# A longer stand-in between the second and third product for the state, in the first chunk of each head's scan

## The chip, the cores and the metric

The kernel runs on one core of a Trainium2 chip. The metric is the device time of one execution in microseconds (us), as a median of several runs. Engine names follow the profile: PE is the matrix engine, PEld its weight loads, DVE the vector engine, ACT the scalar engine, POOL the GpSimd engine, SP the engine that issues most DMAs.

## What is computed

A decoder trunk of two layers over 1024 tokens of width 1024. The first layer is a gated DeltaNet with 8 heads (key width 128, value width 256), the second a sliding-window attention that reads keys and values computed once. Only the first layer is touched here. Its core is a scan over chunks of the sequence that carries a state S:

```python
def step(S, inp):
    qk_i, qd_i, kd_i, u_i, w_i, gl_i = inp
    v_new = u_i - jnp.einsum("bhck,bhkv->bhcv", w_i, S)
    o = jnp.einsum("bhck,bhkv->bhcv", qd_i, S) + jnp.einsum("bhcs,bhsv->bhcv", qk_i, v_new)
    S = S * gl_i[..., None, None] + jnp.einsum("bhck,bhcv->bhkv", kd_i, v_new)
    return S, o
```

Everything around it in that layer is projection work: the layer's input, normalised, times the weights for queries, keys, values and a gate z, then a short convolution along the sequence, and at the end a product with the output weights.

## The kernel before

The sequence is cut into 8 chunks of 128 tokens. Factors of the scan and the projections are split into a high and a low part, and three products (high by high, low by high or high by low, and the other cross product) stand for one product in full precision.

The first layer goes head by head, heads 0 to 7. `head_delta` (L658) is the scan of one head. Its first half builds, for all 8 chunks at once, the inverse that the chunked form needs: products of keys with queries (L668), a mask, levels of small products (L700, L693), three corrections (L693), three merges (L762, L767, L772). Its second half is the loop over chunks n (L796 to L838): r from the state (L800, L802; not in the first chunk, which has no state yet), the new values from r (L809), their high part `vh` on ACT (L811) and their low part `vl` on DVE (L812, tile lh), three products for the new state (L820 and L821 with `vh`, L823 with `vl`), S itself on DVE (L829 in the first chunk, L826 later), its high and low parts (L831, L832). `inside` (L785; its products are L654 to L656, as are those of L815) computes the output of a chunk.

These steps form one long chain for a head, so the PE would stand idle between them. The kernel fills it: `head_delta` is a generator that yields, after each step, a number from the table `WAIT`, roughly the microseconds that its next step has to wait for the other engines. `interleave` (L86) then issues projection matmuls of the next head and of the gate (`gemm_ct`, lines L180, L182, L184, called fillers here) until their costs (0.215 to 0.22 each) add up to that number times `share`. `share` (L348) is the projection work of the head over `WAIT_SUM`, the sum of all that a head yields; so the number of fillers of a head is fixed, and the table only says how they are spread. Heads 5 and 6 leave their gate's projection to the end, and head 0 has half of its gate done earlier, so they have fewer fillers per step than heads 1 to 4 and 7.

The order on the PE is the order in which the program is written. On DVE, ACT, POOL and SP a scheduler sets the order from its own estimate of when each operation's inputs are there; each engine then runs its list strictly in order. On DVE the scan shares the list with the low parts of weights (L157), the three taps of a convolution (L494), the key norms (L589 to L591, L111 to L119), the sums for the queries (L546, L548), and the low parts of the decayed keys and of the decay (L648: tile lt and tile dml; the high parts are POOL's L647).

Of the kernel before, what the change touches and what calls it, by code (L numbers as in the profile page):

```python
# [24 lines left out]
NEG = -1.0e30  # L25
EPS = 1e-6

WAIT = {"kq": 0.7, "mask": 4.05, "level": 1.37, "fix": 2.05, "merge": 1.04, "row": 0.99, "new": 1.02, "state": 0.86, "low": 0.23}
WAIT_SUM = 4 * WAIT["kq"] + 1 * WAIT["mask"] + 10 * WAIT["level"] + 3 * WAIT["fix"] + 3 * WAIT["merge"] + 7 * WAIT["row"] + 8 * WAIT["new"] + 7 * WAIT["state"] + 7 * WAIT["low"]
LEVELS = (1, 2, 4, 8, 16, 32)  # L30

C_ID = 0
# [32 lines left out]
class Kernel:  # L65
# [190 lines left out]
    def layer_a(self):  # L256
        nc, tc, I = self.nc, self.tc, self.I
        with ExitStack() as ctx:
# [76 lines left out]
            for h in range(AH):  # L335
# [11 lines left out]
                spare = 0.99 if h in late else 6 if h + 1 == AH else 10  # L347
                share = (10.4 * blocks - spare) / WAIT_SUM  # L348
                self.interleave(self.head_delta(h, cur), self.chain(back), share)
# [308 lines left out]
    def head_delta(self, h, H):  # L658
        nc, dl, sm, dps = self.nc, self.dl, self.sm, self.dps
        kq, kt, vt, dm = H.kq, H.kt, H.vt, H.dm  # L660
# [3 lines left out]
        for n2 in range(NB // 2):  # L664
            ps = dps.tile([P, 2, 2, P], F32, name="kqp")
            for c in range(2):
                n = n2 * 2 + c
                nc.tensor.matmul(ps[:, c, :, :], kq[:, n, 0, :], kq[:, n, :, :], start=True, stop=True)  # L668
            for c in range(2):
                n = n2 * 2 + c  # L670
# [3 lines left out]
            nc.vector.tensor_tensor(out=dm[:, sl, :], in0=ps[:, :, 1, :], in1=dm[:, sl, :], op=ALU.mult)  # L674
            yield WAIT["kq"]

# [13 lines left out]
        def prod(lhs, rhs):  # L690
            ps = dps.tile(sh, F32, name="kqp")
            for n, r in blocks:
                nc.tensor.matmul(ps[r:r + 64, n, :], lhs(n, r), rhs(n, r), start=True, stop=True)  # L693
            return ps
# [8 lines left out]
        def part(t):  # L703
            return lambda n, r: t[r:r + 64, n, :]

        def const(j):
            return self.mskh[:, 64 * j:64 * j + 64].unsqueeze(1).broadcast_to(sh)

        def swap(name, t):
            o = sm.tile(sh, F16, name=name, bufs=1)  # L710
            nc.vector.transpose(out=o.rearrange("p n c -> p (n c)"), in_=t.rearrange("p n c -> p (n c)"))
            return o
# [7 lines left out]
        XT = swap("XT", X)  # L720
        yield WAIT["mask"]
        pair = [P, 2, NB, 64]
        w = sm.tile(pair, F32, name="w0", bufs=1)
        Xf, XTf = w[:, 0], w[:, 1]
        for lv, b in enumerate(LEVELS[1:], 2):
            y = whole(self.lh, X)
            Z = sm.tile(sh, F16, name="Z", bufs=1)
            nc.vector.tensor_tensor(out=Z, in0=y, in1=const(lv), op=ALU.mult)
            yield WAIT["level"]
            px = prod(part(XT), part(Z))  # L730
# [3 lines left out]
            else:  # L734
                pxt = prod(part(Z), part(XT))
                nc.vector.tensor_tensor(out=Xf, in0=px, in1=X, op=ALU.add)
                nc.vector.tensor_tensor(out=XTf, in0=pxt, in1=XT, op=ALU.add)
            yield WAIT["level"]

# [6 lines left out]
        for t in (Eh, Ef):  # L746
            nc.vector.tensor_tensor(out=t, in0=y, in1=Ef, op=ALU.add)
        yield WAIT["fix"]
        y = prod(part(Eh), part(XTh))
# [35 lines left out]
        def inside(n):  # L785

            self.three(po[n % 2][:, 1, :], dmh[:, n, :], dml[:, n, :], vh, vl)
            if n:
                nc.vector.tensor_tensor(out=o[:, n, :], in0=po[n % 2][:, 1, :], in1=o[:, n, :], op=ALU.add)
            else:  # L790
                nc.scalar.copy(out=o[:, n, :], in_=po[n % 2][:, 1, :])
            junk = sm.tile([P, 256], BF16, name="junk2", bufs=1)
            nc.scalar.activation(out=junk, in_=o[:, n, :], func=AF.Square, accum_out=sso[:, n:n + 1])

        S = None
        for n in range(NB):  # L796
            po[n % 2] = dps.tile([P, 2, 256], F32, name="kqp")
            if n:
                ps = dps.tile([P, 512], F32, name="sc")[:, 0:256]
                nc.tensor.matmul(ps, kq[:, n, 0, :], S, start=True, stop=True)  # L800
                r = sm.tile(wide, F32, name="r")
                nc.vector.scalar_tensor_tensor(out=r, in0=ps, scalar=self.neG[:, n, h:h + 1], in1=vt[:, n, :],  # L802
                                               op0=ALU.mult, op1=ALU.add)
                inside(n - 1)
                yield WAIT["row"]
            else:
                r = vt[:, n, :]
            ps = dps.tile([P, 512], F32, name="sc")[:, 0:256]
            nc.tensor.matmul(ps, xt[:, n, :], r, start=True, stop=True)  # L809
            beta = self.beta[:, n, h:h + 1]  # L810
            nc.scalar.activation(out=vh, in_=ps, func=AF.Copy, scale=beta)  # L811
            nc.vector.scalar_tensor_tensor(out=vl, in0=ps, scalar=beta, in1=self.f32(vh), op0=ALU.mult,  # L812
                                           op1=ALU.subtract)
            if n:
                self.three(po[n % 2][:, 0, :], qh[:, n, :], ql[:, n, :], Sh, Sl)  # L815
                nc.scalar.activation(out=o[:, n, :], in_=po[n % 2][:, 0, :], func=AF.Copy, scale=self.eG[:, n, h:h + 1])
            yield WAIT["new"]
            if n < NB - 1:
                ps = dps.tile([P, 512], F32, name="sc")[:, 0:256]
                nc.tensor.matmul(ps, kth[:, n, :], vh, start=True, stop=False)  # L820
                nc.tensor.matmul(ps, ktl[:, n, :], vh, start=False, stop=False)  # L821
                yield WAIT["low"]
                nc.tensor.matmul(ps, kth[:, n, :], vl, start=False, stop=True)  # L823
                S2 = sm.tile(wide, F32, name="S")
                if n:
                    nc.vector.scalar_tensor_tensor(out=S2, in0=S, scalar=self.egl[:, n, h:h + 1], in1=ps,  # L826
                                                   op0=ALU.mult, op1=ALU.add)
                else:
                    nc.vector.tensor_copy(S2, ps)  # L829
                S = S2  # L830
                nc.scalar.copy(out=Sh, in_=S)  # L831
                nc.vector.tensor_tensor(out=Sl, in0=S, in1=self.f32(Sh), op=ALU.subtract)  # L832

                if n < 4:
                    (part_d, part_k, part_d, part_d)[n](some[(0, 1, 1, 2)[n]])
                if n == 2:
                    part_k(some[2])
                yield WAIT["state"]  # L838
# [560 lines left out]
```

## Time and profile before

| | |
|---|---|
| median of 3 runs | 1867.74 us (1866.12 to 1868.64) |
| the profiled execution | 1867.72 us |
| its span, first to last instruction | 1866.0 us |
| scans of the 8 heads, in the span | about 99 us to 890 us |
| PE busy in the span | 97% |

The profile comes from one execution, of 1867.72 us; 1.7 us of it lie outside the span. In rows of the timeline the first two numbers are the start in us from the span's start and the length; a row with xN is N equal instructions in one piece, and [1.19 <-DVE lh L812] says that the engine stood idle for 1.19 us before it, until DVE's L812 released it. Idle time under about 0.2 us has no bracket.

### The profile page before, as it was taken

How to read it: one execution, taken by the hardware profiler on the slowest of the kernel's cores; microseconds unless marked ns; L12 is line 12 of the kernel's file. 1: busy time of each engine (PE TensorE's matmuls, PEld its weight loads, DVE VectorE, ACT ScalarE, POOL GpSimd, SP SyncE). 2: the span in 40 equal slices, each digit the busy share in tenths (PEclk: the TensorE clock that was granted, in tenths of full speed). 3: DMA queues.
4: the chain of work that ended last, by engine and by line, in shares of the span. 5: the costliest groups of instructions: out<-in, count | busy, mean ns of one | idle time of the engine just before them, and what ended most of it. 6: DMA issues, size and time to landing. Idle time of an engine off the chain costs nothing.

```text
span 1866.0 us, 31106 instructions
## 1 busy us (share of the span) xinstructions
PE 1809.7 (97%) x11778; PEld 1466.0 (79%) x11778; DVE 1231.2 (66%) x2895; ACT 730.7 (39%) x1813; POOL 514.0 (28%) x629
## 2 busy tenths in 40 slices
PE   6999999999999998999999999999999999999999
PEld 6667778787878776778788899887787787777887
DVE  6777776868586778765545365777776766763432
ACT  6446362634445364523112042444444444441100
POOL 1323232323222233221311231333333323221211
PEclk9999999999999999999999999999999999999999
DMA  4611111112011111122655331111111111225552
GB/s 151 134 49 35 57 46 46 47 35 69 23 58 35 58 34 47 45 91 92 236 170 171 122 92 46 30 46 46 63 41 52 57 34 59 68 69 201 182 169 102
DMA packets 134874, 149.55 MB, mean 80 GB/s; under 512 B 7242, under 2 KB 91716, under 8 KB 134724
## 3 DMA queue, kind: packets, MB, share of 16 engines
q1 hardware_dynamic: 124384, 130.40, 22.5%
q10 hardware_dynamic: 10340, 17.16, 2.9%
q8 instruction: 93, 1.52, 0.3%
q14 instruction: 57, 0.47, 0.1%
HBM read 116.05 MB, written 31.49 MB: 79 GB/s over the span
## 4 chain that ended last, share of the span: by engine, by line
PE 77%; DVE 10%; issue 3%; POOL 3%; ACT 1%; DMA 1%; POOLq 0%; DVEq 0%; ACTq 0%; SPq 0%
PE mm L180 9%; PE mm L182 9%; PE mm L184 9%; PE acc L933 6%; PE acc L932 6%; PE acc L931 6%; PE mm L983 4%; PE mm L984 4%; PE mm L985 4%; PE pv L1218 3%; PE lg L1174 3%; DVE acc L494 2%; PE tp L1197 1%; DVE wlo L157 1%; PE kqp L693 1%
## 5 line engine op out<-in xcount | busy, mean ns | idle before, releaser
L180 PE MATMUL mm<-hh,whi 128*128 128x512 f32 (+1 forms) x1040 | 428.0, 412 | 2.5 <-ACT hh L246 2.4
L182 PE MATMUL mm<-hl,whi 128*128 128x512 f32 (+1 forms) x1040 | 417.9, 402 | 1.5 <-DVE hl L247 1.5
L184 PE MATMUL mm<-hh,wlo 128*128 128x512 f32 (+1 forms) x1040 | 415.4, 399 | 0.0
L157 DVE TENSOR_TENSOR wlo<-wraw,whi 128x512 fp32r<-128x512 f32 x292 | 205.8, 728 | 225.0 <-POOL whi L150 192.4
L150 POOL TENSOR_SCALAR whi<-wraw 128x1024 fp32r<-128x1024 f32 x110 | 121.3, 1103 | 474.7 <-PE acc L933 240.7
L180 PEld LDWEIGHTS mm<-hh,whi 128*128 128x128 f32 x1040 | 197.0, 189 | 39.1 <-issue 4.6
L184 PEld LDWEIGHTS mm<-hh,wlo 128*128 128x128 f32 x1040 | 196.9, 189 | 37.3 <-issue 4.2
L182 PEld LDWEIGHTS mm<-hl,whi 128*128 128x128 f32 x1040 | 197.2, 190 | 35.6 <-issue 4.2
L983 PE MATMUL mm<-whi,hh 128*128 128x256 f32 x608 | 183.6, 302 | 0.0
L984 PE MATMUL mm<-wlo,hh 128*128 128x256 f32 x608 | 171.9, 283 | 0.0
L985 PE MATMUL mm<-whi,hl 128*128 128x256 f32 x608 | 171.8, 283 | 0.0
L494 DVE SCALAR_TENSOR_TENSOR acc<-u,cw,acc 128x512 f32<-128x512 f32 x192 | 152.9, 798 | 22.0 <-POOL acc L491 19.6
L1187 ACT ACTIVATE lsb<-lsb,m 128x129 f32<-128x129 f32 x256 | 100.4, 394 | 165.2 <-DVE m L1182 129.3
L983 PEld LDWEIGHTS mm<-whi,hh 128*128 128x128 f32 x608 | 115.8, 190 | 14.7 <-issue 10.0
L1191 POOL TENSOR_TENSOR lsb<-lsb,den 128x512 f32<-128x512 f32 x64 | 72.9, 1139 | 189.2 <-DVE den L1189 177.6
L153 POOL TENSOR_TENSOR wraw<-wraw,gcolb 128x512 f32<-128x512 f32 x72 | 79.0, 1117 | 140.4 <-DMA wraw<-in_b_w_in 96.7
L984 PEld LDWEIGHTS mm<-wlo,hh 128*128 128x128 f32 x608 | 116.1, 191 | 0.2
L985 PEld LDWEIGHTS mm<-whi,hl 128*128 128x128 f32 x608 | 115.8, 190 | 0.0
L491 POOL TENSOR_SCALAR acc<-u,cw 128x512 f32<-128x512 f32 x64 | 57.0, 891 | 183.4 <-ACT u L487 169.9
L931 PE MATMUL acc<-whi,hh 128*128 128x512 f32 x256 | 99.7, 389 | 0.0
L933 PE MATMUL acc<-whi,hl 128*128 128x512 f32 x256 | 99.6, 389 | 0.0
L932 PE MATMUL acc<-wlo,hh 128*128 128x512 f32 x256 | 99.6, 389 | 0.0
(352 smaller groups left out, 3722.0 us busy)
## 6 DMA issues: line engine op xcount, KB each, us to landing
wraw<-in_a_w_in SPq DMA_DIRECT2D x48, 512.0 KB, 4.0
wraw<-in_a_w_out SPq DMA_DIRECT2D x32, 512.0 KB, 3.6
wraw<-in_b_w_in SPq DMA_DIRECT2D x32, 512.0 KB, 4.0
wraw<-in_b_w_out SPq DMA_DIRECT2D x32, 512.0 KB, 3.9
og<-zs SPq DMA_DIRECT2D x32, 256.0 KB, 2.0
ogT<-zs SPq DMA_DIRECT2D x24, 256.0 KB, 2.1
btab<-lt SPq DMA_DIRECT2D x1, 4096.0 KB, 24.3
dm<-gd SPq DMA_DIRECT2D x8, 512.0 KB, 4.1
```

The lines of the kernel that those rows point to most:

```text
L150: nc.gpsimd.tensor_scalar(out=hi, in0=raw, scalar1=1.0, scalar2=1.0, op0=ALU.mult, op1=ALU.mult)
L157: nc.vector.tensor_tensor(out=lo[:, ks], in0=raw[:, ks], in1=self.f32(hi[:, ks]), op=ALU.subtract)
L180: nc.tensor.matmul(ps, hi[:, k, :], hh[:, k, :], start=(k == 0), stop=False)
L182: nc.tensor.matmul(ps, hi[:, k, :], hl[:, k, :], start=False, stop=False)
L184: nc.tensor.matmul(ps, lo[:, k, :], hh[:, k, :], start=False, stop=(k == KT - 1))
L494: nc.vector.scalar_tensor_tensor(out=acc, in0=u[:, t:t + 512], scalar=cw[:, t, blk:blk + 1], in1=acc, op0=ALU.mult, op1=ALU.add)
L931: nc.tensor.matmul(ps[c], oh[:, k, ts], hi[:, kk, :], start=(k4 + k == 0), stop=False)
L932: nc.tensor.matmul(ps[c], oh[:, k, ts], lo[:, kk, :], start=False, stop=False)
L933: nc.tensor.matmul(ps[c], ol[:, k, ts], hi[:, kk, :], start=False, stop=(k4 + k == 6))
L983: nc.tensor.matmul(ps, hh[:, k, ts], hi[:, k % 4, :], start=(k == 0), stop=False)
L984: nc.tensor.matmul(ps, hh[:, k, ts], lo[:, k % 4, :], start=False, stop=False)
L985: nc.tensor.matmul(ps, hl[:, k, ts], hi[:, k % 4, :], start=False, stop=(k == KT - 1))
```

## The change

`WAIT` gets a new entry, `low0` = 1.5. In the loop over chunks, between L821 and L823, the first chunk yields it instead of `low` = 0.23; the other six still yield `low`. `WAIT_SUM` counts 6 times `low` and once `low0`, so it goes from 52.54 to 53.81, and `share` falls by 2.4% in every head.

```diff
-WAIT = {..., "state": 0.86, "low": 0.23}
-WAIT_SUM = ... + 7 * WAIT["state"] + 7 * WAIT["low"]
+WAIT = {..., "state": 0.86, "low": 0.23, "low0": 1.5}
+WAIT_SUM = ... + 7 * WAIT["state"] + 6 * WAIT["low"] + WAIT["low0"]
...
                 nc.tensor.matmul(ps, kth[:, n, :], vh, start=True, stop=False)
                 nc.tensor.matmul(ps, ktl[:, n, :], vh, start=False, stop=False)
-                yield WAIT["low"]
+                yield WAIT["low" if n else "low0"]
                 nc.tensor.matmul(ps, kth[:, n, :], vl, start=False, stop=True)
```

Both programs hold the same instructions on every engine; they differ in order between head 0's scan and the end of head 7's, and nowhere else. Three places follow.

On the PE, head 5, first chunk, before: from the first product for the state to the first use of the state (L800). The operands are Z for `vh`, lh for `vl`, w_7089 and lt for the high and low part of the keys.

```order
L820 MATMUL sc<-Z,w_7089 128x256
L821 MATMUL sc<-Z,lt 128x256
L823 MATMUL sc<-lh,w_7089 128x256
L180 MATMUL mm<-hh_85,whi 128x512
L182 MATMUL mm<-hl_86,whi 128x512
L184 MATMUL mm<-hh_85,wlo 128x512
L800 MATMUL sc<-S,kq 128x256
```

The same place after:

```order
L820 MATMUL sc<-Z,w_7086 128x256
L821 MATMUL sc<-Z,lt 128x256
L180 MATMUL mm<-hh_85,whi 128x512
L182 MATMUL mm<-hl_86,whi 128x512
L184 MATMUL mm<-hh_85,wlo 128x512
L180 MATMUL mm<-hh_85,whi 128x512
L182 MATMUL mm<-hl_86,whi 128x512
L823 MATMUL sc<-lh,w_7086 128x256
L184 MATMUL mm<-hh_85,wlo 128x512
L180 MATMUL mm<-hh_85,whi 128x512
L182 MATMUL mm<-hl_86,whi 128x512
L800 MATMUL sc<-S,kq 128x256
```

Five fillers stand before L823 where there were none; three of them were taken from steps ahead of L820 (111 fillers of the head stood ahead of L820, now 108) and two from steps behind.

On DVE, head 5, the list up to the first state (L829), before:

```order
L157 TENSOR_TENSOR wlo<-wraw,whi 128x512
L591 TENSOR_TENSOR kt<-kt,rky 128x1024
L648 TENSOR_TENSOR lt<-kt,w_7089 128x256 x2
L648 TENSOR_TENSOR lt<-kt,w_7089 128x512
L648 TENSOR_TENSOR dml<-dm,w_7091 128x256 x2
L494 SCALAR_TENSOR_TENSOR acc<-u,cw,acc 128x512
L648 TENSOR_TENSOR dml<-dm,w_7091 128x512
L812 SCALAR_TENSOR_TENSOR lh<-sc,beta,Z 128x256
L494 SCALAR_TENSOR_TENSOR acc<-u,cw,acc 128x512
L829 COPY S<-sc 128x256
```

After:

```order
L591 TENSOR_TENSOR kt<-kt,rky 128x1024
L648 TENSOR_TENSOR lt<-kt,w_7086 128x256 x2
L648 TENSOR_TENSOR lt<-kt,w_7086 128x512
L648 TENSOR_TENSOR dml<-dm,w_7088 128x256 x2
L494 SCALAR_TENSOR_TENSOR acc<-u,cw,acc 128x512
L812 SCALAR_TENSOR_TENSOR lh<-sc,beta,Z 128x256
L494 SCALAR_TENSOR_TENSOR acc<-u,cw,acc 128x512
L648 TENSOR_TENSOR dml<-dm,w_7088 128x512
L829 COPY S<-sc 128x256
```

One L157 and the last L648 no longer stand ahead of L812; the L648 now stands between L812 and L829, the L157 behind L829.

On the PE, head 1 (heads 2 to 4 are the same), the merges, before; L596 turns the next head's keys:

```order
L762 MATMUL kqp<-cst,xt 64x64 x8
L180 MATMUL mm<-hh_87,whi 128x512
L182 MATMUL mm<-hl_88,whi 128x512
L184 MATMUL mm<-hh_87,wlo 128x512
L596 MATMUL tr<-cst,kt 128x128 x8
L180 MATMUL mm<-hh_87,whi 128x512
L182 MATMUL mm<-hl_88,whi 128x512
L767 MATMUL kqp<-w_2148,lt 64x64 x8
```

After:

```order
L762 MATMUL kqp<-cst,xt 64x64 x8
L182 MATMUL mm<-hl_88,whi 128x512
L184 MATMUL mm<-hh_87,wlo 128x512
L180 MATMUL mm<-hh_87,whi 128x512
L182 MATMUL mm<-hl_88,whi 128x512
L767 MATMUL kqp<-w_2147,lt 64x64 x8
L184 MATMUL mm<-hh_87,wlo 128x512
L596 MATMUL tr<-cst,kt 128x128 x8
```

L596 is behind L767 now, since it hangs on the number of fillers issued. On POOL, at the same place of head 1, before (L686 decays the next head's keys and waits for L596; L647 splits this head's keys and decay):

```order
L686 TENSOR_TENSOR kt<-kt,kdec 128x512 x2
L647 TENSOR_SCALAR w_2682<-kt 128x256 x2
L647 TENSOR_SCALAR w_2682<-kt 128x512
L647 TENSOR_SCALAR w_2684<-dm 128x256 x2
L647 TENSOR_SCALAR w_2684<-dm 128x512
```

After:

```order
L647 TENSOR_SCALAR w_2679<-kt 128x256 x2
L647 TENSOR_SCALAR w_2679<-kt 128x512
L686 TENSOR_TENSOR kt<-kt,kdec 128x512 x2
L647 TENSOR_SCALAR w_2681<-dm 128x256 x2
L647 TENSOR_SCALAR w_2681<-dm 128x512
```

L686 has moved from ahead of both splits to between them.

## Rows read from the trace of the kernel before

**Rows 1.** The page's head and first part: busy us, share of span, instructions

```profile
span 1866.0 us, 31106 instructions
PE 1809.7 (97%) x11778; PEld 1466.0 (79%) x11778; DVE 1231.2 (66%) x2895; ACT 730.7 (39%) x1813; POOL 514.0 (28%) x629
```

**Rows 2.** A stretch: length, busy us (PE, PEld, DVE, ACT, POOL), PEclk, DMA

```profile
750.00:755.00 5.00, 2.78 (x10) 2.27 (x10) 3.99 (x8) 2.21 (x3) 0.00 (x0) 0.76 0.61 206
```

**Rows 3.** The PE's waits over the span: us in total, times, longest us

```profile
PE sc L823 <- DVE lh L812: 10.8, 14, 2.2
```

**Rows 4.** Timeline of PE, first chunk: heads 0, 1, 5 (five rows), 6, 7

```profile
147.46 0.39 PE L823 MATMUL sc<-lh,w 128*128 128x256 f32 x1 [1.19 <-DVE lh L812]
...
251.40 0.37 PE L823 MATMUL sc<-lh,w 128*128 128x256 f32 x1
...
658.16 0.39 PE L184 MATMUL mm<-hh,wlo 128*128 128x512 f32 x1
658.39 0.28 PE L820 MATMUL sc<-Z,w 128*128 128x256 f32 x1
...
660.89 0.39 PE L823 MATMUL sc<-lh,w 128*128 128x256 f32 x1 [2.10 <-DVE lh L812]
...
661.89 0.70 PE L800 MATMUL sc<-S,kq 128*128 128x256 f32 x2
...
752.24 0.39 PE L823 MATMUL sc<-lh,w 128*128 128x256 f32 x1 [2.22 <-DVE lh L812]
...
846.65 0.38 PE L823 MATMUL sc<-lh,w 128*128 128x256 f32 x1 [0.80 <-DVE lh L812]
```

**Rows 5.** Timeline of DVE, head 5, first chunk

```profile
653.66 0.69 DVE L157 TENSOR_TENSOR wlo<-wraw,whi 128x512 fp32r<-128x512 f32 x1
...
659.64 0.68 DVE L648 TENSOR_TENSOR dml<-dm,w 128x512 fp32r<-128x512 f32 x1
660.36 0.48 DVE L812 SCALAR_TENSOR_TENSOR lh<-sc,beta,Z 128x256 fp32r<-128x256 f32 x1
660.76 0.74 DVE L494 SCALAR_TENSOR_TENSOR acc<-u,cw,acc 128x512 f32<-128x512 f32 x1
661.41 0.42 DVE L829 COPY S<-sc 128x256 f32<-128x256 f32 x1
```

**Rows 6.** Timeline of POOL, head 5: the high parts of the decay

```profile
656.67 2.12 POOL L647 TENSOR_SCALAR w<-dm 128x256 fp32r<-128x256 f32 x3
```

**Rows 7.** Timeline, second chunk's start: PE in head 5, DVE and PE in head 6

```profile
663.70 0.59 PE L809 MATMUL sc<-r,xt 128*128 128x256 f32 x2
...
752.76 0.42 DVE L829 COPY S<-sc 128x256 f32<-128x256 f32 x1
...
753.66 1.05 PE L800 MATMUL sc<-S,kq 128*128 128x256 f32 x2
...
756.46 0.59 PE L809 MATMUL sc<-r,xt 128*128 128x256 f32 x2
```

**Rows 8.** Timeline, head 5's third chunk, and L494 over the span (ns min/median/max)

```profile
669.27 3.26 DVE L494 SCALAR_TENSOR_TENSOR acc<-u,cw,acc 128x512 f32<-128x512 f32 x3
...
672.98 0.38 PE L823 MATMUL sc<-lh,w 128*128 128x256 f32 x1 [1.30 <-DVE lh L812]
...
L494 DVE SCALAR_TENSOR_TENSOR acc<-u,cw,acc x192: 706/743/1601, 35.0 to 798.2; 128x512 f32<-128x512 f32 x192
```

**Rows 9.** Timeline of PE, third chunk of head 0

```profile
156.05 0.70 PE L800 MATMUL sc<-S,kq 128*128 128x256 f32 x2 [1.57 <-DVE S L826]
```

**Rows 10.** Timeline, head 1: PE and POOL in the merges, PE in chunk 2

```profile
242.60 1.04 PE L596 MATMUL tr<-cst,kt 128*128 128x128 f32 x8
...
243.29 2.52 POOL L686 TENSOR_TENSOR kt<-kt,kdec 128x512 f32<-128x512 f32 x2 [0.78 <-PE tr L596]
...
256.93 0.39 PE L820 MATMUL sc<-Z,w 128*128 128x256 f32 x1 [0.45 <-ACT Z L811]
```

**Rows 11.** Timeline of DVE, head 7: the low parts of the keys

```profile
840.59 2.80 DVE L648 TENSOR_TENSOR lt<-kt,w 128x256 fp32r<-128x256 f32 x3 [3.90 <-POOL w L647]
```

More of the change, by code (lines that the diff above doesn't have):

```diff
@@ L26 @@
 EPS = 1e-6
-WAIT = {"kq": 0.7, "mask": 4.05, "level": 1.37, "fix": 2.05, "merge": 1.04, "row": 0.99, "new": 1.02, "state": 0.86, "low": 0.23}
-WAIT_SUM = 4 * WAIT["kq"] + 1 * WAIT["mask"] + 10 * WAIT["level"] + 3 * WAIT["fix"] + 3 * WAIT["merge"] + 7 * WAIT["row"] + 8 * WAIT["new"] + 7 * WAIT["state"] + 7 * WAIT["low"]
+WAIT = {"kq": 0.7, "mask": 4.05, "level": 1.37, "fix": 2.05, "merge": 1.04, "row": 0.99, "new": 1.02, "state": 0.86, "low": 0.23, "low0": 1.5}
+WAIT_SUM = 4 * WAIT["kq"] + 1 * WAIT["mask"] + 10 * WAIT["level"] + 3 * WAIT["fix"] + 3 * WAIT["merge"] + 7 * WAIT["row"] + 8 * WAIT["new"] + 7 * WAIT["state"] + 6 * WAIT["low"] + WAIT["low0"]
 LEVELS = (1, 2, 4, 8, 16, 32)
```

## The prediction, made before the changed kernel ran

> **What bounds the kernel now.** I read the page's first part, then the PE's waits, then the timelines of PE, DVE and POOL at the first chunk of each head, then stretches for the clock. The page says that the PE is the bound: 97% of the span busy, DVE at 66% [rows 1]. So what an edit can win here is time in which the PE stands idle, and it wins it only if the PE does not stand idle later instead. The longest entry among the PE's waits is the one that the edit aims at: L823 waits for `vl` (DVE's L812) 10.8 us in 14 places [rows 3]. At the first chunk it waits 1.19 us in head 0, 2.10 in head 5, 2.22 in head 6 and 0.80 in head 7, and in head 1 not at all [rows 4]; heads 2 to 4 look like head 1. That is 6.31 us. The rest lies in other chunks, where the number of fillers per step stays what it was, give or take one.
>
> The next question is what L812 itself waits for. In head 5 DVE is busy without a gap from L157 to L829: the low parts of the decay, L812, a tap, then S [rows 5]. So the PE waits there for a DVE that is behind, and S, the next thing the PE needs, comes out of the same queue: S is done at 661.83 (661.41 + 0.42) and L800 starts at 661.89 [rows 4, 5]. That decides the reading of this change: more fillers ahead of L823 let the PE do work in the wait, but S comes no earlier for it. A wait that disappears at L823 can come back at L800.
>
> **The change, part by part.** A filler takes 0.23 us (658.16 to 658.39 [rows 4]). With `low0` the first chunk gets 5 fillers ahead of L823 in heads 0, 5 and 6 (1, 0 and 0 before) and 7 in heads 1 to 4 and 7 (2 and 1 before), by the order of the two programs. All of a head's fillers are issued before its end in both, so a head's time changes by its PE waits alone, and the right account at any point is: how much earlier is the PE there, plus 0.23 for each filler that it has done more. At L800 of the second chunk the PE has done 2 more in heads 0, 5, 6 and 7 (head 5: 116 against 114): a credit of 0.46 us.
>
> Head 5. On DVE's list the L157 (0.69) has gone from ahead of L812 to behind L829, and one L648 (0.68) from ahead of L812 to between L812 and L829 [rows 5]. L812 could thus come up to 1.4 earlier, S only up to 0.7. POOL sets a floor: its split of the decay ends at 658.79 (656.67 + 2.12 [rows 6]) and starts after a merge on the PE, which has two fillers fewer ahead of it (0.46). So S comes between 0 and 0.7 earlier; I take 0.4, about POOL's 0.46. With the credit that is 0.9 (ends 0.46 and 1.2). I expect a wait of some 0.5 left at L823 and one of some 0.7 new at L800, in place of 2.10. In the third chunk L823 waits 1.30 behind three taps that took 3.26 together, 1.09 each [rows 8]; the new DVE list has two taps ahead of that L812 and the third between it and S. That is worth between 0 (S is as late as before) and 1.09; three fillers stand between L823 and L800 and hide 0.7 of the tap that now follows, so I take 0.4. Head 5: 1.3.
>
> Head 6 has the same wait, and it costs more than it shows. Behind it the granted clock falls: 0.76 in the mean of 750 to 755, which is a mixture of the two levels, 2.4 and 1.2 GHz [rows 2]. From L800 to L809 of the second chunk head 5 takes 1.81 us (661.89 to 663.70) and head 6, with the same instructions, 2.80 (753.66 to 756.46) [rows 4, 7]; and the three fillers ahead of L800 were slow as well, so that L800 came 0.48 after S was done (752.76 + 0.42 = 753.18 against 753.66 [rows 7]). With five fillers inside the wait the longest idle piece shrinks from 2.22 to about 1. Head 5 kept full speed behind 2.10, as its 1.81 shows, so I take it that head 6 will too. S itself comes no earlier: on DVE the L157 only moves from ahead of L812 to between L812 and S. So 0.48 + 0.99 + 0.46 of credit = 1.9. If the clock falls again, only the credit and a little of the 0.48 are left: 0.5.
>
> Of the clock, the Trainium skill ("TensorE: Matmul & The Clock Gate", What's actually happening) says that the slow state is the default and activity releases it. That agrees with the 0.76 behind the longest wait. By it the clock could also fall at another place where waits are added; no row here shows where.
>
> Head 7. DVE has time here: it stood idle 3.90 us before the low keys, which wait for POOL, and POOL for a merge on the PE [rows 11]. Three fillers fewer stand ahead of that merge, so the whole DVE chain starts 0.7 earlier, and six more fillers (1.4) lie ahead of L823. The wait of 0.80 goes, and S is early enough for L800. I take 0.7 (ends 0.3 and 0.8).
>
> Head 0. The wait is 1.19, but DVE is behind here as in head 5, and between L812 and S two operations stand now (a tap and an L157) where one L648 stood. S comes at the same time or 0.2 earlier; with the credit 0.5. Then the third chunk: L800 waits 1.57 for S [rows 9]. The new DVE list has one tap ahead of that S instead of two, but that tap needs a POOL operation (L491) that now stands behind an L686, which POOL takes as soon as L596 is done. Ends: 0.7 lost to 1.6 won on top of the 0.5; I take a loss of 0.3. Head 0: 0.2.
>
> Heads 1 to 4 have nothing to win at L823. They lose two to three fillers ahead of the merges (0.46 to 0.7), where DVE is behind; this can turn into a wait of about that size. It is given back at L820 of the second chunk, which waits 0.45 for ACT [rows 10] and which the PE now reaches two fillers later. I take 0 for each; the ends are plus and minus 0.46, so 1.8 either way for the four.
>
> The sum is 1.3 + 1.9 + 0.7 + 0.2 = 4.1 us, all of it from first-chunk waits but the 0.4 and the 0.3. Against the profiled execution, 1867.72, that gives 1863.6; the median of the runs, 1867.74, is the same number. Nothing behind the first layer is reordered, and its chain starts from head 7's end, so the gain is carried to the end in full. SP's queue keeps its order but for one pair of neighbouring loads early in the layer.
>
> **The rivals.**
> The wait only moves. If POOL and DVE give S at the old time in heads 0 and 5, and head 6's clock falls all the same, what is left is some credit: 0.3 in head 5, 0.5 in head 6, 0.5 in head 7, nothing in head 0. Gain 1.3, time 1866.4. For it: DVE without a gap in rows 5, and S just in time for L800. Against it: the L157 that has left the queue.
>
> All of it comes. If DVE has made up its arrears by the time the PE is through the five fillers, 1.19 + 2.10 + 2.22 + 0.80 go, and with the clock's 0.99 and the third chunk's 0.4 that is 7.7: 1860.0. Against it: S would have to come 1.2 to 2.1 us earlier than its queue allows.
>
> Slower: heads 1 to 4 lose at the merges. L596 stood ahead of L767 and stands behind it now, and POOL's L686 (2.52 us, released by L596 [rows 10]) has moved between the two splits of L647. The split of the decay, and behind it three L648 and L812, then wait for L596: about 1.3 us later (L767's 1.1 and a filler). The five added fillers (1.15) and the two transposes ahead of L823 should just cover it. If they don't, and if the fillers missing ahead of the merges (0.7) are waited for too, a head loses 1.9, four heads 7.6, against the 4.1 won: 1871.2. The point from which this decides is a loss of 1.0 in each of the four heads. Against it: POOL's keys now come 2.5 us earlier, so the sum of POOL's work up to the decay is the same.
>
> DVE gets slower. A tap takes 0.74 as a rule and up to 1.60 [rows 8], and the long ones lie beside POOL's L686 in the timeline; with POOL's list moved, other operations of DVE will lie beside it. Each new meeting costs up to 0.86 (1.60 less 0.74); two in each of heads 0, 5 and 6, all on the way to S, cost 5.2, more than the 4.1, and give 1868.8. Against it: as many old meetings can go, and the list of POOL holds the same work. Of this the Trainium skill ("SBUF — State Buffer", SBUF: two separate sides) says that a GpSimd operation and a DVE operation with two inputs from SBUF lock each other out for a whole instruction; the 1.60 of a tap that has two such inputs agrees.
>
> **How the numbers follow.** The forecast, most of head 6's clock and half of head 5's wait won: 0.50, 1863.6, own range 1861.5 to 1865.5 from the ends above. The wait only moves: 0.26. All of it: 0.12. Slower, 0.12: the merges 0.06, DVE's meetings with POOL 0.06. What a measurement of this kernel can tell from no change is about 0.2%, 3.7 us, so "faster" means below 1864.0. The forecast lies just beyond that line: about 0.31 of its 0.50 are faster and 0.19 the same. With all of "all of it" faster is 0.43; the same is 0.19 + 0.26 + 0.04, since 1868.8 is within 0.2%, 0.49; slower is the merges' 0.06 and 0.02 of still longer meetings, 0.08. The range reaches from the case of "all of it" to a little above the time before, with the tail of the slower case left out: 1860.0 to 1868.8.
>
> **What would show it.** In the profile after: L823 of the first chunk waits under 1.2 us in heads 5 and 6 and not in heads 0 and 7; L800 of the second chunk waits 0.4 to 0.9 for S in heads 5 and 6, where it did not wait; the granted clock stays at 1.00 through head 6; L494 in head 5's third chunk releases L812 some 1 us earlier; heads 1 to 4 keep their length to 0.5 us. The prediction is wrong if the waits at L800 are as long as those that went (the wait moved), if L812 in heads 1 to 4 is released by POOL's L647 (slower), or if the clock falls at a new place.

## The result and the profile after

The changed kernel takes 1879.87 us in the median of four runs (1878.55 to 1881.97), the kernel before 1867.79 beside it. The ratio is 1.0063, with a 95% interval from 1.0048 to 1.0077: 12 us slower, where 4 us faster was forecast and 1868.8 was the upper end of the range. The profiled execution of after took 1880.09 us, its span is 1878.4.

The page's head and first part, which answer to [rows 1]:

```profile
span 1878.4 us, 31114 instructions
PE 1813.6 (97%) x11778; PEld 1463.0 (78%) x11778; DVE 1230.8 (66%) x2895; ACT 728.6 (39%) x1813; POOL 516.6 (28%) x629
```

The same instructions run, and DVE and ACT are busy no longer than before. The span is 12.4 us longer, the PE's busy time 3.9. So most of the loss, 8.5 us, is idle time of the PE. The PE's waits over the span of after (total us, times, longest), to be read against [rows 3]:

```profile
PE sc L809 <- DVE r L802: 5.5, 12, 1.2
PE sc L820 <- ACT Z L811: 4.8, 4, 1.2
PE sc L823 <- DVE lh L812: 4.7, 6, 2.0
PE kqp L700 <- DVE X L732: 4.3, 7, 0.9
PE sc L800 <- DVE S L826: 4.2, 7, 1.2
...
PE sc L800 <- DVE S L829: 1.6, 4, 0.5
...
PE kqp L693 <- DVE Z L747: 0.8, 4, 0.2
```

The edit did what it aims at: L823 waits 4.7 us in place of 10.8. But before had 0.8 us at L809 where after has 5.5, 2.5 at L820 against 4.8, 2.7 at L700 (for L732) against 4.3, 1.9 at L800 (for L826) against 4.2, and nothing at L693 for L747 or at L800 for L829.

Where does it happen? For every step that is no filler I took its time from the head's first L668, less the same time in before, less 0.23 us for each filler that after has done more by then (plus 0.23 for each that it has done fewer). An example: L820 of the first chunk in head 1 starts at 250.16 in before, 52.28 behind the head's start at 197.88, with 142 fillers done; in after at 252.49, 53.72 behind 198.77, with 139 done. That is 53.72 - 52.28 + 3 x 0.23 = 2.13 us late. The table has this lateness at three points: the first L809 (all that lies ahead of the scan), L821 of the first chunk, and the head's end.

| head | 0 | 1 | 2 | 3 | 4 | 5 | 6 | 7 | sum |
|---|---|---|---|---|---|---|---|---|---|
| first L809 | 0.54 | 0.80 | 0.78 | 0.74 | 0.83 | 0.57 | 0.35 | 0.44 | 5.05 |
| L821, first chunk | 0.34 | 2.21 | 2.23 | 2.17 | 2.27 | 0.61 | -0.01 | 0.45 | 10.27 |
| end of the head | 0.80 | 2.81 | 2.01 | 2.77 | 2.83 | 0.40 | 2.39 | -0.26 | 13.75 |

10.3 of the 13.75 us are lost before L823 of the first chunk, the place of the edit, is reached; 1.35 come back behind head 7 and were not followed. There are two losses ahead of it: about 0.6 us in every head in front of the scan, and 1.4 more in heads 1 to 4 at L820.

The first, in the timeline of PE in head 1: of before, then of after.

```profile
219.19 0.39 PE L700 MATMUL kqp<-X,lhd 128*128 128x64 f16 x8 [0.45 <-DVE X L732]
...
235.01 0.44 PE L693 MATMUL kqp<-XT,Z 64*64 64x64 f16 x16
```

```profile
220.08 0.39 PE L700 MATMUL kqp<-X,lhd 128*128 128x64 f16 x8 [0.70 <-DVE X L732]
...
235.82 0.44 PE L693 MATMUL kqp<-XT,Z 64*64 64x64 f16 x16 [0.20 <-DVE Z L747]
```

Both steps come at the same distance from the head's start (21.31 and 21.31 us; 37.13 and 37.05), because DVE sets it, but after has done one filler fewer at the first (56 against 57) and three fewer at the second (102 against 105). The wait is 0.25 longer at the first, where it was one already, and new at the second. A filler that is missing in front of a wait is 0.23 us lost.

The second, at the merges and L820 of head 1 in after (POOL, DVE, ACT, PE):

```profile
245.44 1.53 POOL L647 TENSOR_SCALAR w<-kt 128x256 fp32r<-128x256 f32 x3 [1.82 <-issue]
...
246.94 2.23 POOL L686 TENSOR_TENSOR kt<-kt,kdec 128x512 f32<-128x512 f32 x2
...
247.01 1.25 DVE L648 TENSOR_TENSOR lt<-kt,w 128x256 fp32r<-128x256 f32 x1
...
248.19 1.53 DVE L494 SCALAR_TENSOR_TENSOR acc<-u,cw,acc 128x512 f32<-128x512 f32 x1
...
250.44 0.88 DVE L494 SCALAR_TENSOR_TENSOR acc<-u,cw,acc 128x512 f32<-128x512 f32 x1
...
251.35 0.63 ACT L575 ACTIVATE acc<-acc 128x512 f32<-128x512 f32 x1 [2.15 <-DVE acc L494]
...
251.89 0.46 ACT L811 ACTIVATE Z<-sc,beta 128x256 fp32r<-128x256 f32 x1
...
252.49 0.36 PE L820 MATMUL sc<-Z,w 128*128 128x256 f32 x1 [1.17 <-ACT Z L811]
```

The end of the same chain in before (DVE, ACT, PE):

```profile
247.51 0.74 DVE L494 SCALAR_TENSOR_TENSOR acc<-u,cw,acc 128x512 f32<-128x512 f32 x1
...
248.28 0.64 ACT L575 ACTIVATE acc<-acc 128x512 f32<-128x512 f32 x1
...
249.43 0.47 ACT L811 ACTIVATE Z<-sc,beta 128x256 fp32r<-128x256 f32 x1 [0.52 <-PE sc L809]
...
250.16 0.28 PE L820 MATMUL sc<-Z,w 128*128 128x256 f32 x1
```

L596 stands behind L767 now, so L686, which it releases, comes behind the split of the keys and not ahead of it [rows 10]. There it lies beside an L648 and a tap of DVE that take 1.25 and 1.53 us; the L648 of the same shape just before took 0.61, and a tap takes 0.74 as a rule [rows 8]. The tap is one of those that ACT's L575 waits for. L811 stands behind L575 in ACT's list, and so the PE waits for a `vh` whose own input has long been there. Heads 2 to 4 have the same rows (waits of 1.17 to 1.21).

Then the places that the forecast spoke of: L823 of the first chunk and L800 of the second in heads 0, 5, 6 and 7 of after. They answer to [rows 4].

```profile
147.91 0.39 PE L823 MATMUL sc<-lh,w 128*128 128x256 f32 x1 [0.77 <-DVE lh L812]
...
149.50 0.70 PE L800 MATMUL sc<-S,kq 128*128 128x256 f32 x2 [0.37 <-DVE S L829]
...
672.13 0.38 PE L823 MATMUL sc<-lh,w 128*128 128x256 f32 x1 [0.92 <-DVE lh L812]
...
673.73 0.70 PE L800 MATMUL sc<-S,kq 128*128 128x256 f32 x2 [0.53 <-DVE S L829]
...
764.25 0.38 PE L823 MATMUL sc<-lh,w 128*128 128x256 f32 x1 [2.03 <-DVE lh L812]
...
765.85 1.22 PE L800 MATMUL sc<-S,kq 128*128 128x256 f32 x2 [0.51 <-DVE S L829]
...
860.97 0.32 PE L823 MATMUL sc<-lh,w 128*128 128x256 f32 x1
...
862.43 0.70 PE L800 MATMUL sc<-S,kq 128*128 128x256 f32 x2 [0.22 <-DVE S L829]
```

The wait at L823 is shorter everywhere (1.19, 2.10, 2.22 and 0.80 before), and a wait for S stands at L800 in all four heads, where none stood. In head 6 it hardly shrank: the three fillers missing ahead of L820 bring the PE there 0.70 us earlier, and `vl` comes 0.26 later.

### The profile page after: what moved, and what is told of

It reads as the page before. It is cut to its first block, busy times and chain, and to the rows that moved or that the text cites. A ratio compares the mean times of both kernels' runs of the same rounds, so it can differ in the third digit from the quotient of the medians.

```text
span 1878.4 us, 31114 instructions
## 1 busy us (share of the span) xinstructions
PE 1813.6 (97%) x11778; PEld 1463.0 (78%) x11778; DVE 1230.8 (66%) x2895; ACT 728.6 (39%) x1813; POOL 516.6 (28%) x629
## 3 DMA queue, kind: packets, MB, share of 16 engines
q8 instruction: 93, 1.52, 0.3%
## 4 chain that ended last, share of the span: by engine, by line
PE 70%; DVE 11%; issue 7%; POOL 3%; ACT 3%; DMA 1%; POOLq 0%; ACTq 0%; DVEq 0%; SPq 0%
PE mm L180 8%; PE mm L182 8%; PE mm L184 8%; PE acc L932 6%; PE acc L933 6%; PE acc L931 6%; PE mm L983 4%; PE mm L984 4%; PE mm L985 4%; PE pv L1218 3%; PE lg L1174 3%; DVE acc L494 3%; PE tp L1197 1%; DVE wlo L157 1%; PE kqp L693 1%
## 5 line engine op out<-in xcount | busy, mean ns | idle before, releaser
L157 DVE TENSOR_TENSOR wlo<-wraw,whi 128x512 fp32r<-128x512 f32 x292 | 202.9, 719 | 224.2 <-POOL whi L150 190.8
L494 DVE SCALAR_TENSOR_TENSOR acc<-u,cw,acc 128x512 f32<-128x512 f32 x192 | 151.1, 789 | 25.5 <-POOL acc L491 24.1
```

The lines of the kernel that those rows point to most:

```text
L157: nc.vector.tensor_tensor(out=lo[:, ks], in0=raw[:, ks], in1=self.f32(hi[:, ks]), op=ALU.subtract)
L494: nc.vector.scalar_tensor_tensor(out=acc, in0=u[:, t:t + 512], scalar=cw[:, t, blk:blk + 1], in1=acc, op0=ALU.mult, op1=ALU.add)
```

## Experiments

Theory S: the loss comes from `share`, which the larger WAIT_SUM lowers by 2.4% for every step of a head. Theory L: it comes from the five fillers that the first chunk gets, behind which the scan's chain is late. Then, within S, whether the wait at L820 is a matter of order (O) or of missing fillers (F), and whether the order hurts through DVE's speed (M) or its queue alone (Q).

### The share alone

```diff
-                yield WAIT["low" if n else "low0"]
+                yield WAIT["low"]
```

This is the changed kernel with the old yield; WAIT_SUM stays at 53.81.

> Only the smaller share: WAIT_SUM as in the changed kernel (53.81), but the first chunk yields 0.23 as before, so that no step has more fillers ahead of it and every step has 2.4% fewer; the fillers left over (5 or 6 a head) run behind the scan. Theory S (the loss comes from the fillers that are missing ahead of the scan): the waits on DVE ahead of the scan grow by 0.5 to 0.7 us a head as in the changed kernel (5.0 us over eight heads), L596 stands behind L767 in heads 1 to 4, L820 of the first chunk waits 1.2 for ACT there, and nothing is won at L823 of the first chunk in heads 5 to 7: 1878 to 1884 us, as slow as the changed kernel or slower. Theory L (the loss comes from the five added fillers, behind which the scan's chain is late): within 3 us of the time before, 1866 to 1871 us.

Measured: 1886.07 us, ratio 1.0098 [1.0084, 1.0112]; 17 us slower than before, 6 slower than the changed kernel, and above the 1884 that S had given as its upper end. In heads 1 to 4 the lateness is 0.79 to 0.84 at the first L809 and 2.20 to 2.29 at L821, as in the changed kernel to 0.05 us, with L820 waiting 1.2. That is S: the loss needs no longer wait in the first chunk. The PE's waits of this run:

```profile
PE sc L823 <- DVE lh L812: 15.0, 14, 2.9
```

15.0 in place of 10.8 in before: with fewer fillers the PE comes to L823 earlier. What the edit's five fillers do is to take part of that back. Head 7 is 2.0 late at its first L809, where it was 0.4 in the changed kernel; this was not followed.

### The longer wait alone

```diff
-... + 6 * WAIT["low"] + WAIT["low0"]
+... + 7 * WAIT["low"]
```

This is the changed kernel with the old sum; only this number differs from it.

> Only the longer wait: the first chunk yields 1.5, WAIT_SUM stays at 52.54, so that the steps ahead of the scan have as many fillers as before, L823 of the first chunk and all steps behind it have 5 to 7 more, and the fillers run out 5 or 6 early at the end of a head's scan. Theory S: heads 1 to 4 have L596 ahead of L767 as before, no wait at L820 of the first chunk above that of before, and the waits at L823 of heads 0, 5, 6 and 7 shrink as in the changed kernel: 1862 to 1868 us. Theory L: heads 1 to 4 lose 2 us each and the time is 1874 to 1880 us.

Measured: 1871.11 us, ratio 1.0012 [1.0003, 1.0021]. One number in the sum is worth 0.5%. Ahead of the scan nothing is late in heads 0 to 5 (between -0.14 and -0.02 at the first L809), and L820 of the first chunk does not wait in heads 1 to 4. So the two large losses are the share's. But S had expected 1862 to 1868, and this is 2.4 us slower than before. Head 0 is 2.6 shorter, head 5 0.5; heads 1 to 4 are 0.3 to 0.8 longer, head 6 1.6 (it was 2.9 late when it entered its scan: 1.4 came in waits at L668 and L700, the rest with a fall of the granted clock at 714.3) and head 7 3.9. Part of it is seen at head 1's second chunk, in the timeline of PE:

```profile
250.32 0.28 PE L823 MATMUL sc<-lh,w 128*128 128x256 f32 x1
...
251.99 0.70 PE L800 MATMUL sc<-S,kq 128*128 128x256 f32 x2 [0.47 <-DVE S L829]
```

The five fillers put L823 off where it did not wait [rows 4], and S, which needs it, is late at L800. In head 7 1.5 us are lost ahead of the scan, in waits of L668 and L700 for DVE, whose list the fillers moved in head 6.

### The wait paid for behind it

```diff
-WAIT = {..., "state": 0.86, ...
+WAIT = {..., "state": 0.86 - 1.27 / 7, ...
```

The changed kernel, with 1.27 taken from the seven state steps, so that WAIT_SUM is 52.54 again. In the second kernel this is done in heads 0, 5, 6 and 7 alone.

> The wait of 1.5 is paid for behind it: each of the seven state steps yields 1.27/7 less, so that WAIT_SUM and the share stay as before, the first chunk gets its 5 fillers in every head, and the later chunks have as many done by chunk 6 as before. Theory S: nothing changes ahead of the scan, heads 1 to 4 keep their length to 0.5 us, heads 5 to 7 win 1 to 2 us together: 1863 to 1868 us. Theory L: heads 1 to 4 lose 2 us each: 1873 to 1880 us.

> As the kernel with the wait paid for behind it, but in heads 0, 5, 6 and 7 alone, where L823 of the first chunk waits; heads 1 to 4 have the order of before. Theory S: 1863 to 1867 us, 1 to 4 us won at L823 of heads 0, 5, 6 and 7, and heads 1 to 4 as long as before. Theory L: 1866 to 1870 us, the wait at L823 only moves to L800 and L809 of the second chunk.

Measured: 1871.37 us, ratio 1.0014 [1.0005, 1.0023], and 1870.21 us, ratio 1.0008 [0.9998, 1.0019]. Heads 1 to 4 keep their length to 0.1 us in the second and lose 0.0 to 0.7 in the first; nothing is late ahead of their scan. In the first this is against L, which expected 2 us a head. But S's gain at L823 is not there either, and for the second kernel L's account, that the wait only moves (1866 to 1870), fits better than S's 1863 to 1867. In the second kernel head 5 is 1.2 ahead at L823 of the first chunk and 1.2 behind at L809 of the third; head 7 is 1.2 ahead at L800 of the second chunk and, after a wait of 1.85 for S there in the third, 0.8 behind. The wait moved; and the later chunks, which paid, miss the fillers. Head 6 lost 2.7 in both, 1.5 of it ahead of its scan, where the granted clock fell. Head 0 won 1.1 in the first; in the second it lost 0.5, with 1.6 lost ahead of its scan, where the clock fell.

### The order of L596 and L686

```diff
-        self.later(18, lambda: g(0))
-        self.later(18, lambda: g(1))
+        self.later(17, lambda: g(0))
+        self.later(17, lambda: g(1))
```

These lines in `keys_normed` issue L596; the number counts ticks, one for every three fillers. With 17 in the changed kernel, L596 stands ahead of L767 again in heads 1 to 4 and L686 ahead of the split of the keys; with 19 in the kernel before, both stand as in the changed kernel. The fillers of all other steps stay.

> The changed kernel, but L596 (and with it POOL's L686) is issued one filler's tick earlier, so that in heads 1 to 4 L596 stands ahead of L767 and POOL's L686 ahead of the split of the keys, as in the kernel before; the number of fillers at every step is that of the changed kernel. Theory O (the new wait of 1.2 us at L820 of the first chunk in heads 1 to 4 comes from the order of L596 and L686, which put L686 beside DVE's work on the way to L811): the wait of 1.2 goes in four heads, 1.4 each, 5.6 us: 1872 to 1876 us. Theory F (it comes from the three fillers that are missing ahead of it, so that the PE is there too early): as the changed kernel, 1878 to 1881 us.

> The kernel before, but L596 is issued one tick later, so that in heads 1 to 4 it stands behind L767 and POOL's L686 between the two splits, as in the changed kernel; fillers, WAIT_SUM and all yields are those of before. Theory O: L820 of the first chunk waits about 1.2 us for ACT in heads 1 to 4 and the time rises by 3 to 6 us: 1871 to 1875 us. Theory F: with no filler missing there is no new wait: 1866 to 1870 us.

Measured: the changed kernel with L596 early 1874.75 us, ratio to before 1.0035 [1.0023, 1.0047]; the kernel before with L596 late 1877.16 us, ratio 1.0044 [1.0032, 1.0057]. L820 of the first chunk in head 1, of the first and of the second:

```profile
253.13 0.28 PE L820 MATMUL sc<-Z,w 128*128 128x256 f32 x1
```

```profile
254.32 0.36 PE L820 MATMUL sc<-Z,w 128*128 128x256 f32 x1 [1.20 <-ACT Z L811]
```

O holds both ways. With L596 early the lateness of heads 1 to 4 at L821 is what it was at L809 (0.76 to 0.88): the 1.4 is gone, and what remains is the fillers' part. With L596 late it is zero at L809 and 1.42, 1.42, 1.35 and 1.44 at L821, with not one filler fewer. The totals fit less well than the heads. The first kernel won back 5 us where heads 1 to 4 won 6.4: head 0, whose L596 moved as well, lost 1.9 and head 5 0.5, and head 6 won 1.6. The second rose by 8 to 9 us, above the 3 to 6 expected: the four heads account for 5.5, head 5, where L596 moved too, for 2.0, and its first head began 3.0 us later, while head 6 won 0.8. L596 moved ahead of the first head too: it put ACT's L597 behind L575 in ACT's list, and the PE's L436 waits 2.22 us for it there; the granted clock then is 0.50 from 79.9 to 83.3.

### L686 made short

```diff
-nc.gpsimd.tensor_tensor(out=kt[:, hs], in0=kt[:, hs], ...broadcast_to([P, 4, P]),
+nc.gpsimd.tensor_tensor(out=kt[:, hs, 0:16], in0=kt[:, hs, 0:16], ...broadcast_to([P, 4, 16]),
```

> The kernel with L596 one tick later, and of POOL's L686 only 16 of 128 columns are scaled, so that L686 is short; the rest of the scaling of the keys is left out. DVE's, ACT's and PE's lists are those of the kernel with L596 later, row by row. Theory M (L686 slows the DVE operations that run beside it, 1.25 and 1.53 us where 0.61 and 0.74 are usual, 1.4 us on the way to the acc that ACT's L575 waits for, and L811 stands behind L575): those operations take 0.6 and 0.75, and the wait of 1.2 at L820 of the first chunk goes in heads 1 to 4 (under 0.2). Theory Q (the queue alone: DVE's L494 stands behind two L648 in the new order): the DVE operations get shorter, but L820 still waits over 0.8.

This is the kernel with L596 late; it leaves out most of the scaling of the keys. Measured in a single execution: 1866.46 us. Head 1 in its timeline (POOL, DVE, ACT, PE):

```profile
246.88 0.73 POOL L686 TENSOR_TENSOR kt<-kt,kdec 128x64 f32<-128x64 f32 x2
...
246.95 0.51 DVE L648 TENSOR_TENSOR lt<-kt,w 128x256 fp32r<-128x256 f32 x1
...
247.38 0.78 DVE L494 SCALAR_TENSOR_TENSOR acc<-u,cw,acc 128x512 f32<-128x512 f32 x1
...
248.68 0.95 DVE L494 SCALAR_TENSOR_TENSOR acc<-u,cw,acc 128x512 f32<-128x512 f32 x1
...
249.67 0.63 ACT L575 ACTIVATE acc<-acc 128x512 f32<-128x512 f32 x1 [0.53 <-DVE acc L494]
...
250.37 0.48 ACT L811 ACTIVATE Z<-sc,beta 128x256 fp32r<-128x256 f32 x1
...
251.10 0.29 PE L820 MATMUL sc<-Z,w 128*128 128x256 f32 x1
```

The L648 takes 0.51 in place of 1.25, the tap 0.78 in place of 1.53: 1.5 us, which is the 1.4 that a head had lost. L820 does not wait, and heads 1 to 4 are as long as in before (to 0.23 us), with DVE's, ACT's and PE's lists the same row by row as in the kernel with L596 late. So M: the order hurts because L686 slows what lies beside it on DVE; the queue alone costs nothing here. L686's shorter time on POOL is changed too, but the rows that got shorter are DVE's.

The Trainium skill ("SBUF — State Buffer", SBUF: two separate sides) says that a GpSimd operation that reads SBUF and a DVE operation with two inputs from SBUF exclude each other for a whole instruction. L686 and L648 both have two such inputs, and the 1.25 against 0.51 agrees. These rows do not show whether the exclusion lasts a whole instruction.

### More share

```diff
-WAIT_SUM = ... + 7 * WAIT["low"]
+WAIT_SUM = ... + 7 * WAIT["low"] - 1.27
```

In the kernel before, with its own yields.

> The other sign of the share: WAIT_SUM 51.27, 2.4% more fillers at every step, first chunk as before; the fillers run out 5 early at the end of a head's scan. Theory S as a slope (each filler that stands ahead of a wait in front of the scan saves its 0.23): the waits ahead of the scan shrink by 0.3 to 0.7 us a head, 1862 to 1867 us. Theory T (the share of before is where the waits ahead of the scan are just covered, and more fillers only make the chain late): 1867 to 1873 us, no gain ahead of the scan, and waits for S or r at L800 and L809 grow.

Measured: 1880.66 us, ratio 1.0061 [1.0049, 1.0073]. T, and by more than its 1873. The slope has no sign: 2.4% fewer fillers cost 17 us (some 5.7 of them in heads 1 to 4 through the order of L596), 2.4% more cost 12. Heads 1 to 4 are 1.4 to 1.6 late at the first L809 though they have done three fillers more. One reason, head 1 (DVE, then PE):

```profile
233.22 0.69 DVE L157 TENSOR_TENSOR wlo<-wraw,whi 128x512 fp32r<-128x512 f32 x1
...
233.83 0.68 DVE L747 TENSOR_TENSOR Z<-kqp,w 128x512 f16<-128x512 f32 x1
...
234.57 0.44 PE L693 MATMUL kqp<-XT,Z 64*64 64x64 f16 x16 [0.70 <-DVE Z L747]
```

The fillers need their own weights' low parts sooner, and an L157 now stands ahead of the L747 for which the PE waits.

### The longer wait in two heads

```diff
-                yield WAIT["low"]
+                yield WAIT["low0" if n == 0 and h in (0, 5) else "low"]
```

In the kernel before, with its sum (7 times 0.23).

> The longer wait of the first chunk in heads 0 and 5 alone, with WAIT_SUM and share of before; the other heads have the fillers of before. In the run with the longer wait alone head 0 took 2.6 us less than before and head 5 0.5 less. Theory K (these heads' gain is a gain of their own): 2 to 3 us faster, 1865 to 1866.5 us. Theory N (head 0's gain came from the execution, or goes again behind it): within 1 us of the time before, 1867 to 1869.5 us.

Measured: 1865.24 us, ratio 0.9979 [0.9970, 0.9988]: 4 us faster than before beside it (1869.70), faster than both kernels. By the expectation's times it is K, by the gain a little above its 2 to 3. In its trace head 0 is 0.8 us shorter although a fall of the clock in its front (0.59 from 105.1 to 109.1) cost it 1.6, and head 5 is 0.5 shorter; heads 1 to 4 and 7 keep their length to 0.1 us. That would be 2.9 of the 4. But head 6, whose fillers are those of before, is 2.8 longer, and 1.4 of it is there before its clock falls at 713.4. At the end of head 5 a DVE split for the queries (L648, tile ql) takes 1.52 us, where before it took 0.68, and head 6's L668 waits 0.90 for the L789 behind it; in the kernel with the longer wait alone it is the same. So the trace shows about 1.5 us won by the edit. The gain of the runs goes with the clock as well: nine of these twelve have a mean granted clock of 0.997 or 0.998, two of the 17 of before do; among runs with the same mean clock, some of them single, the kernel is 1 to 2.6 us faster. Whether the edit is what keeps the clock higher stays open.

## Why the prediction was wrong

**What bounds the kernel** was right, idle time of the PE, and in the main so was the rule that a head's time changes by its waits alone (8.5 of the 12.4 us; 3.9 are longer busy time of the same instructions). The step that failed first is the sentence that the rest lies in other chunks, where the number of fillers per step stays what it was, give or take one. I read the change at the place where it adds fillers. It takes them from all other steps, by 2.4%, and the "one" adds up to three per head in front of the scan. They stood ahead of waits for DVE that were in the trace of before (L700 waits 0.45 in head 1) or just covered (L693). Not in the sum: 5.05 us.

**Heads 1 to 4: 0 each** is the term with the largest error: they lost 10.4 us. I had bounded it by 0.46 either way, by fillers missing at the merges. 3.2 us are lost ahead of the scan; 5.7 come from L686 beside DVE; 1.5 arise later. The rival "slower: heads 1 to 4 lose at the merges" had the right order of L596, L767 and L686, the right heads and a point of decision, 1.0 a head, that was passed. Its path was wrong: not the split of the decay and L812 were late, but the tap, L575 and through ACT's list L811. The slowing had been in the other rival, as a new meeting of DVE and POOL, at up to 0.86 each; the two operations measured 0.64 (1.25 less 0.61) and 0.79 (1.53 less 0.74) more. I gave the two 0.06 each, because I asked of each alone whether it could eat 4 us, and put the meetings in heads 0, 5 and 6, not where L686 had moved. The argument against it, that POOL's sum of work up to the decay is the same, says nothing of what lies beside it.

**Head 5**: 1.3 forecast, -0.4 measured. The first chunk went as described: 0.92 left at L823 and 0.53 new at L800 (some 0.5 and 0.7 forecast), and from L809 of the first chunk to L800 of the second it won 0.5 (0.57 late to 0.04). But it entered the scan 0.57 late, and the third chunk's gain (L823 waits 0.58 in place of 1.30) was gone by L800 and L809 of the fifth.

**Head 6**: 1.9 forecast, -2.4 measured. L823 waits 2.03, and the clock fell again, where [rows 2] has 0.76:

```profile
766.00:771.00 5.00, 5.00 (x22) 4.31 (x22) 2.78 (x8) 2.64 (x8) 0.00 (x0) 0.72 0.44 120
```

0.72 is again a mixture of 1.2 and 2.4 GHz. From L800 to L809 of the second chunk after takes 3.32 us, before 2.80. That more fillers in the wait keep the clock was the term of 0.99, and the runs speak against it: in the kernels with the wait paid for, L823 of head 6 waits 1.06 and 1.07 us, about the 1 that was forecast, and the clock fell behind it in both (0.66 from 755 to 760 in the second). With the longer wait alone, which waits 1.06 too, it stayed. The largest loss of head 6 is another one, 1.5 us between L809 of the second chunk and of the third (POOL, DVE, PE):

```profile
772.91 2.28 POOL L686 TENSOR_TENSOR kt<-kt,kdec 128x512 f32<-128x512 f32 x2 [0.74 <-PE tr L596]
...
773.00 1.27 DVE L832 TENSOR_TENSOR XT<-S,X 128x256 fp32r<-128x256 f32 x1
...
774.20 1.53 DVE L494 SCALAR_TENSOR_TENSOR acc<-u,cw,acc 128x512 f32<-128x512 f32 x1
...
776.18 0.70 PE L809 MATMUL sc<-r,xt 128*128 128x256 f32 x2 [1.22 <-DVE r L802]
```

L596 comes ahead of this chunk's L800 now and behind it in before, so L686 lies beside an L832 (0.42 in before) and a tap that stand ahead of L802 in DVE's list. It is the meeting of heads 1 to 4 once more, at another place; no experiment separates it here.

**Head 7**: 0.7 forecast, 0.3 measured at its last chunk; the first chunk's wait went as said. **Head 0**: 0.2 forecast, -0.8 measured, 0.54 of it ahead of the scan.

**The wait only moves** came nearest for the edit taken by itself: with the share of before the time is 1871.11, 1871.37 or 1870.21, and it forecast 1866.4; the 1.3 us of credit that it left did not come. In short, what the edit does at its place in all heads came out between nothing and 3 us lost, and what its sum does everywhere else cost the larger part of the 12 us.

## What to carry to other kernels

When a table spreads a fixed amount of cover over many steps, a larger entry at one place is paid by all others: list which of those stand ahead of a wait that exists or is just covered, and add up what each loses, before looking at the place that gains. When such a change moves an operation of one engine past others, ask what it will then run beside, on which path that work lies, and what stands behind it in each in-order list. A number that is tuned in this way can be worse on both sides; here an edit in only the heads that gain, with the sum left alone, was faster.

## What was not expected of the hardware

The clock falls at a few places of this kernel in some executions and not in others, and neither the order on the PE nor the length of the wait ahead decides it alone. With L596 early, head 6 of the changed kernel has the same order on the PE up to L800 and the same wait of 2.0 us at L823, and the clock stays (the stretch behind that wait):

```profile
762.00:767.00 5.00, 5.00 (x32) 4.49 (x33) 3.58 (x9) 3.83 (x10) 0.91 (x3) 1.00 0.43 121
```

There L800 to L809 takes 1.97 us, against 3.32 in after. The kernel with the wait paid for in heads 0, 5, 6 and 7 fell at another place, the front of head 6, where before did not, behind a wait of the same length (1.83 and 1.82 us at the first L700; first that kernel, then before):

```profile
715.00:720.00 5.00, 5.00 (x42) 3.81 (x41) 3.58 (x6) 1.18 (x2) 0.00 (x0) 0.66 0.01 3
```

```profile
714.00:719.00 5.00, 5.00 (x62) 3.61 (x60) 4.13 (x7) 1.21 (x2) 0.00 (x0) 1.00 0.14 52
```

This cost it 1.5 us in the profiled execution. The scatter of the runs goes with it: of the 17 runs of the kernel before beside the last experiment, four with a mean granted clock of 0.994 took 1871.8 us in the mean, eight with 0.995 1869.9, three with 0.996 1867.6, one with 0.997 1867.9 and one with 0.998 1864.7. What makes it fall in one execution and not in the next stays open. So a term of one or two microseconds that rests on a fall of the clock in a single profile, as mine for head 6, is not one that an order of instructions can be credited with.
